# Lockstep head groups in a chunked RWKV-7 scan: 16 heads in two groups, one chunk apart

## The chip, the cores and the metric

The kernel runs on one core of a Trainium2 chip. TensorE (PE) multiplies on a 128 x 128 array, DVE, ACT and POOL work on vectors, SP issues DMAs. Time is device microseconds of one execution; runs of a kernel are compared by their median. TensorE's granted clock is given as a share of 2.4 GHz, so 0.50 is 1.2 GHz.

## The reference

A two-layer decoder trunk: 512 positions, width 1024. The first layer has another mixer and a dense feed-forward part; the second has the RWKV-7 time mixing that the change is about, and eight experts of which each position uses two.

```python
# rwkv7_time_mix: 16 heads of 64; state s is 64 x 64 per head
x = h + dx * mix[i]                      # six token-shifted inputs
r, k, v = xr @ w_r, xk @ w_k, xv @ w_v
w_log = -softplus(-(w0 + tanh(xw @ w1) @ w2)) - 0.5
a = sigmoid(a0 + (xa @ a1) @ a2);  g = sigmoid(xg @ g1) @ g2
kk = normalize(k * k_k);  k = k * (1 + (a - 1) * k_a);  decay = exp(-exp(w_log))
def step(s, (r_t, w_t, k_t, v_t, kk_t, b_t)):
    s = s * w_t[None, :] - (s @ kk_t)[:, None] * b_t[None, :] + v_t[:, None] * k_t[None, :]
    return s, s @ r_t
# then: normalize each head's output, scale and shift, add a bonus (r . k . r_k) v, times g, @ w_o
```

## The kernel before

`rwkv` (L599) runs the recurrence in eight chunks of 64 positions (C), for two head groups (hf = 0 and 1) of eight heads. Inside a chunk the dependence of the positions on each other is a triangular 64 x 64 system per head; its inverse is made ahead of the scan.

*Key stage.* For each of eight column tiles n, `key1` makes the key product and ACT (L789, L790) and DVE (L791, L792) scale it; `sums` (L802) and `key2` normalize; `bonus_z` on POOL (L822) and `bonus` (L829) make the bonus; `key3` decays keys and receptances, with L842 on POOL for tiles 0 to 5 and on DVE for 6 and 7. `flip` multiplies a chunk's keys by their decay to the chunk's end on POOL (L850, four tiles of 128 columns at a time), `flop` transposes the result and stores it for the scan.

*Scores and inverse.* `scores(th)` makes the score products of chunks 4 th to 4 th + 3 (L978). The masks of chunks 0 to 3 are applied as DVE evacuates; those of chunks 4 to 7 by `mask` on POOL (L1002 and L1003, eight pairs). `invert(th)` solves 32 x 32 blocks on DVE, 31 steps of up to four instructions (L1020, L1024) and two transposes (L1027, L1029); it is run a few steps at a time between other work. `merge` joins 32 x 32 blocks to 64 x 64 with 2 x 64 small products (L1045, L1062).

*The scan.* For chunk c (64 positions, on partitions 0 to 63 or 64 to 127 as c is even or odd: its natural half) of one group:

- `step1`: products with the state S (L1159, 4 of 128 columns) and with the values (L1164, one per head) go into one accumulator; ACT copies it to Z (L1169);
- `step2`: one product per head with the inverse (L1177); ACT copies it into the other half of the value tile vu (L1181);
- `step3`: state products (L1193; heads alternate between column halves of the array); DVE adds the decayed state SP (L1199, two per chunk; L1201, a copy, in chunk 0); POOL multiplies S by the next decay to SP (L1206);
- `step4`: output products (L1213); ACT copies the result to Y (L1223).

An f32 product is two records in the trace. `slot(s)` issues the steps one group at a time: group 0 on chunk s, group 1 between chunk s - 1's later steps and chunk s's earlier ones. Behind each step `fill` issues some products of a queue of other work: value products (L883) of the second half until they are done, then gate products (L1262 to L1264), from slot 6 on output products (L1321). Generators of side work (the inverse, the masks, the merge, the norms) advance by one after each step. `norm` normalizes 128 positions of a group: on POOL L1242, L1233 and L1234, on DVE L1236, L1237, L1244, L1252 to L1255, on ACT L1241 and L1245. `load_vu` and `load_kt` fetch the next chunk's values and keys (four and three buffers).

The order in the source is not final: a scheduler orders the instructions of all engines by priorities, and `after` pins one instruction behind another. An accumulator bank holds 512 f32 columns; the kernel rotates through eight.

Of the kernel before, what the change touches and what calls it, by code (L numbers as in the profile page):

```python
# [103 lines left out]
class Trunk:  # L104
# [494 lines left out]
    def rwkv(self, hpool):  # L599
# [502 lines left out]
        for j, _ in enumerate(scores(1)):  # L1102
            run(inv, 3)
            if j < NTT:
                flops(next(v3), 1)
            if j == NTT:
                run(v3)
                for i in range(NTT):
                    t = self.t()
                    nc.scalar.activation(t, pv[i], AF.Copy, scale=cm[:, 0:1])  # L1110
                    nc.sync.dma_start(v_d[i * 128:(i + 1) * 128, 0:512], t)
# [40 lines left out]

        def step1(chains):
            for hf, c in chains:
                p_ = PYZ[hf] = self.ps()
                if c:
                    for j in range(4):
                        n = hf * 4 + j
                        nc.tensor.matmul(p_[:, j * 128:(j + 1) * 128], RK[n].rearrange(flat)[:, c * 128:(c + 1) * 128],  # L1159
                                         Sb[(c - 1) % 2][:, n], start=(j == 0), stop=False, skip_group_check=True)  # L1160
            for hd, hs in enumerate(heads):
                for hf, c in chains:
                    nat, opp = sides(c)
                    mm = nc.tensor.matmul(PYZ[hf][opp, hs], AK[hf][c // 2][nat, hd], VU[hf, c][nat, hs],  # L1164
# [916 lines left out]
```

## Time and profile before

| | |
|---|---|
| Median of 3 runs | 1504.39 us (1502.3 to 1504.78) |
| Profiled execution | 1497.78 us |
| Its span | 1496.1 us |
| Mean granted clock | 0.957 |
| Busy PE / DVE / ACT / POOL | 1418.3 / 987.4 / 796.6 / 334.0 us |
| The scan | 858.3 to 1006.4 us |

Durations in the rows come from the profiled execution. A row of the timeline joins instructions of one line that stand next to each other; its length runs to the modelled end of the last, so the distance from one row's start to the next tells the pace. Idle time in brackets is that of the engine just before, with what ended it. A slot here is the stretch from one group 0 chunk's first state product to the next.

### The profile page before, as it was taken

The numbers are of one execution on the slowest core, as the hardware profiler recorded it, in microseconds if no ns is written. First come the engines' busy times: TensorE is split into PE (matmuls) and PEld (weight loads), VectorE is DVE, ScalarE is ACT, GpSimd is POOL, SyncE is SP. The second block draws the span as 40 slices with busy tenths as digits, with TensorE's granted clock in tenths as the row PEclk, the third lists the DMA queues.
The fourth block names the chain that finished last, engine by engine and source line by source line (L and its number), as shares of the span: only waits on it lengthen the run. The fifth ranks groups of instructions, "written<-read, shape, count | busy, mean of one in ns | idle before, by whom it ended". The sixth has DMA issues, their size and how long they took to land. (4 is left out here: it accounts for less than half of the span.)

```text
span 1496.1 us, 31249 instructions
## 1 busy us (share of the span) xinstructions
PE 1418.3 (95%) x12563; PEld 1121.0 (75%) x12563; DVE 987.4 (66%) x1661; ACT 796.6 (53%) x1262; POOL 334.0 (22%) x357
## 2 busy tenths in 40 slices
PE   7999999999999999999978899898999999999995
PEld 5776788888888444744555569776889989999994
DVE  6643564444444433596767992556899998898894
ACT  4842444322322322495549333334678888888872
POOL 4000002000000013102442612533233323421323
PEclk9999999999999999999989578699999999999998
DMA  4220222232223433242133132236889999999993
GB/s 171 85 71 28 85 85 88 96 99 89 95 99 95 118 104 92 71 159 95 57 106 117 53 103 59 63 124 218 323 283 379 371 396 372 366 366 389 349 342 128
DMA packets 77397, 253.91 MB, mean 170 GB/s; under 512 B 9162, under 2 KB 9290, under 8 KB 77244
## 3 DMA queue, kind: packets, MB, share of 16 engines
q1 hardware_dynamic: 70112, 233.34, 44.4%
q0 software_dynamic: 3136, 10.62, 2.3%
q10 hardware_dynamic: 3996, 7.88, 1.4%
q8 instruction: 100, 1.64, 0.5%
q14 instruction: 53, 0.43, 0.1%
HBM read 235.65 MB, written 16.16 MB: 168 GB/s over the span
## 5 line engine op out<-in xcount | busy, mean ns | idle before, releaser
L226 ACT ACTIVATE whi<-wraw 128x1024 fp32r<-128x1024 f32 x95 | 100.6, 1059 | 269.9 <-PE ps L264 126.0
L264 PE MATMUL ps<-xg,whi 128*128 128x512 f32 x544 | 217.1, 400 | 3.8 <-DVE cs L191 3.4
L263 PE MATMUL ps<-xg,whi 128*128 128x512 f32 x544 | 217.0, 399 | 1.0 <-ACT xg L325 1.0
L265 PE MATMUL ps<-xg,wlo 128*128 128x512 f32 x544 | 216.4, 398 | 0.0
L1741 DVE SCALAR_TENSOR_TENSOR wlo<-eraw,wlo 128x1024 f16<-128x1024 f32 x125 | 154.0, 1232 | 13.7 <-ACT wlo L1740 13.6
L1741 DVE SCALAR_TENSOR_TENSOR whi<-eraw,whi 128x1024 f16<-128x1024 f32 x124 | 152.5, 1230 | 13.7 <-ACT whi L1740 13.4
L227 DVE TENSOR_TENSOR wlo<-wraw,whi 128x1024 fp32r<-128x1024 f32 x95 | 118.6, 1249 | 48.9 <-ACT whi L226 47.7
L1740 ACT ACTIVATE wlo<-eraw 128x1024 f16<-128x1024 f32 x125 | 131.9, 1055 | 20.7 <-PE ps L1820 11.0
L1740 ACT ACTIVATE whi<-eraw 128x1024 f16<-128x1024 f32 x124 | 130.7, 1054 | 15.6 <-PE ps L1820 11.6
L1920 POOL TENSOR_TENSOR hh<-su,hh 128x138 f16<-128x138 f32 (+5 forms) x77 | 82.0, 1066 | 217.7 <-ACT hh L1919 215.6
L1820 PE MATMUL ps<-xe,whi 128*128 128x138 f16 (+6 forms) x704 | 126.8, 221 | 3.6 <-DVE whi L1741 2.9
L1818 PE MATMUL ps<-xe,whi 128*128 128x138 f16 (+6 forms) x704 | 127.7, 221 | 0.0
L1819 PE MATMUL ps<-xe,whi 128*128 128x138 f16 (+6 forms) x704 | 127.5, 221 | 0.0
L1819 PE MATMUL ps<-xe,wlo 128*128 128x138 f16 (+6 forms) x704 | 127.2, 221 | 0.3 <-ACT xe L1610 0.3
L1818 PE MATMUL ps<-xe,wlo 128*128 128x138 f16 (+6 forms) x704 | 127.3, 221 | 0.0
L1820 PE MATMUL ps<-xe,wlo 128*128 128x138 f16 (+6 forms) x704 | 126.7, 220 | 0.4
L264 PEld LDWEIGHTS ps<-xg,whi 128*128 128x128 f32 x544 | 103.0, 189 | 31.1 <-DVE xg L326 6.5
L263 PEld LDWEIGHTS ps<-xg,whi 128*128 128x128 f32 x544 | 103.4, 190 | 25.5 <-ACT xg L325 1.3
L265 PEld LDWEIGHTS ps<-xg,wlo 128*128 128x128 f32 x544 | 103.1, 190 | 24.1 <-issue 0.5
L1820 PEld LDWEIGHTS <-whi 128*128 128x128 f16 x1008 | 97.8, 97 | 8.6 <-DVE whi L1741 5.8
L286 POOL TENSOR_TENSOR tmp<-tmp 128x512 f32<-128x512 f32 x21 | 34.8, 1656 | 300.1 <-ACT tmp L284 247.2
L1820 PEld LDWEIGHTS <-wlo 128*128 128x128 f16 x1016 | 98.6, 97 | 2.4 <-DVE wlo L1741 1.6
(516 smaller groups left out, 3467.9 us busy)
## 6 DMA issues: line engine op xcount, KB each, us to landing
eraw<-in_e_w SPq DMA_DIRECT2D x260, 512.0 KB, 7.3
wraw<-in_ffn_g SPq DMA_DIRECT2D x22, 512.0 KB, 3.4
wraw<-in_ffn_u SPq DMA_DIRECT2D x22, 512.0 KB, 3.3
wraw<-in_ffn_d SPq DMA_DIRECT2D x16, 512.0 KB, 3.6
wraw<-in_w_oo SPq DMA_DIRECT2D x13, 512.0 KB, 3.4
wraw<-in_w_mo SPq DMA_DIRECT2D x8, 512.0 KB, 3.2
wraw<-in_w_rk SPq DMA_DIRECT2D x8, 512.0 KB, 3.3
wraw<-in_w_k SPq DMA_DIRECT2D x8, 512.0 KB, 3.4
```

What stands on the lines that cost most here:

```text
L226: nc.scalar.activation(hi, raw, AF.Copy)
L227: nc.vector.tensor_sub(lo, raw, hi.bitcast(F32))
L263: nc.tensor.matmul(ps, hi[:, j], xh, start=(k == 0), stop=False)
L264: nc.tensor.matmul(ps, hi[:, j], xl, start=False, stop=False)
L265: last = nc.tensor.matmul(ps, lo[:, j], xh, start=False, stop=(k == ktot - 1))
L286: self.nc.gpsimd.tensor_add(sq, sq, parts.pop())
L1740: nc.scalar.activation(w[:, 0], raw, AF.Copy, scale=2048.0)
L1741: low = nc.vector.scalar_tensor_tensor(w[:, 1], raw, 2048.0, w[:, 0], op0=OP.mult, op1=OP.subtract)
L1818: nc.tensor.matmul(ps, w[:, 0, j], x[:, 0, k], start=(k == 0), stop=False)
L1819: nc.tensor.matmul(ps, w[:, 0, j], x[:, 1, k], start=False, stop=False)
L1820: nc.tensor.matmul(ps, w[:, 1, j], x[:, 0, k], start=False, stop=(k == n - 1))
L1920: nc.gpsimd.tensor_sub(hh[:, 1, f], u, hh[:, 0, f])
```

## The change

`slot` becomes a lockstep: in slot s group 0 works on chunk s and group 1 on chunk s - 1, so that their natural halves are opposite, and the products of both alternate head by head in L1178 (value products, was L1164), L1201 (was L1177) and L1237 (was L1213). The value products become a step of their own, `step0`, issued for the next slot's chunks behind `step2`; a product with the identity (L1173) opens their accumulator. `step2` writes both groups into one bank, `step3` (L1217, was L1193) too. There are nine slots instead of eight and a piece. The S adds are now L1223 and L1225, the SP multiply L1230, Z's and VU's copies L1193 and L1205, Y's L1247, the state products L1189.

Fills go in two places of a slot, five and three at a time (two and two in slots 4 and 5, twelve and six in 6 and 7, six and six in 8). The eight mask pairs (now L1018, L1019) leave the start of the scan: they are issued in slots 2 to 6, each behind an SP multiply. In the key stage group 0's key decay is multiplied on ACT (L857, one per tile) instead of POOL; `key3` is split, its last two multiplies becoming `key4`; the L842 multiplies of tiles 4 and 5 go from POOL to DVE; the value preparation runs one key step earlier, and the first inverse two steps at a time instead of three under the second scores.

```diff
-            (nc.gpsimd if n < KD - 2 else nc.vector).tensor_mul(a, a, kk)
+            (nc.gpsimd if n < 4 else nc.vector).tensor_mul(a, a, kk)
+
+        def key4(n):
...
-            nc.gpsimd.tensor_mul(s_, blk, PE[:, n4, c:c + 1].to_broadcast([128, 4, 128]))
+            if hf:
+                nc.gpsimd.tensor_mul(s_, blk, PE[:, n4, c:c + 1].to_broadcast([128, 4, 128]))
+            else:
+                for j in range(4):
+                    nc.scalar.activation(s_[:, j], blk[:, j], AF.Copy, scale=PE[:, j, c:c + 1])
...
-            for k in ((), (0,), (1, 2), (3,), (4, 5), (6,), (7,), ())[n]:
+            for k in ((0,), (1,), (2, 3), (4,), (5, 6), (7,), (), ())[n]:
...
-            nc.gpsimd.tensor_mul(z, z, msk[:, 0:1, :].to_broadcast([128, 8, C]))
+            after(nc.gpsimd.tensor_mul(z, z, msk[:, 0:1, :].to_broadcast([128, 8, C])), turned[0])
...
-            run(inv, 3)
+            run(inv, 2)
...
+        def step0(chains):
+            for hf, c in chains:
+                PYZ[hf, c] = self.ps()
+                nat, opp = sides(c)
+                nc.tensor.matmul(PYZ[hf, c][nat, 0:2], self.ident[nat, opp], self.ident[nat, 0:2], start=True, stop=False,
+                                 skip_group_check=True)
+            for hd, hs in enumerate(heads):
+                for hf, c in chains:
+                    nat, opp = sides(c)
+                    mm = nc.tensor.matmul(PYZ[hf, c][opp, hs], AK[hf][c // 2][nat, hd], VU[hf, c][nat, hs],
+                                          start=(hd == 0), stop=False, skip_group_check=True)
+            return mm
...
-            pu = {hf: self.ps() for hf, c in chains}
+            pu = self.ps()
...
-                    mm = nc.tensor.matmul(pu[hf][opp, hs], NT[i // 2][opp, (i % 2) * 16 + hf * 8 + hd], Z[hf][opp, hs],
+                    mm = nc.tensor.matmul(pu[opp, hs], NT[i // 2][opp, (i % 2) * 16 + hf * 8 + hd], Z[hf][opp, hs],
...
-        def slot(s, gs, count, rate):
-            for f, hf, c in ((step1, 0, s), (step3, 1, s - 1), (step2, 0, s), (step4, 1, s - 1),
-                             (step3, 0, s), (step1, 1, s), (step4, 0, s), (step2, 1, s)):
...
+        def chain(s):
+            return [(hf, s - hf) for hf in range(NH) if 0 <= s - hf < NCH]
+
+        def slot(s, gs, counts, rate):
+            now, nxt = chain(s), chain(s + 1)
...
+            mm = step1(now)
+            for hf, c in nxt:
+                load_vu(hf, c)
+                load_kt(hf, c)
+            fill(mm, counts[0])
+            side()
+            mm = step2(now)
+            if nxt:
+                mm = step0(nxt)
+            side()
+            fill(mm, counts[1])
+            step3(now)
+            side()
+            mm = step4(now)
+            side()
+            fill(mm, counts[2])
...
+            run(mk, (0, 0, 1, 2, 2, 2, 1, 0, 0)[s])
-            if s == 1:
+            if s == 4:
                 fill(None, 96 - vdone[0])
...
-            slot(s, ([inv, mk], [inv, mk], [inv, mk], [join], [norms[0, 0], norms[0, 1]], [norms[1, 0], norms[1, 1]], [norms[2, 0]], [norms[2, 1]], [norms[3, 0]])[s],
-                 (2, 1, 1, 1, 1, 1, 4, 4, 4)[s], 1)
+            slot(s, ([inv], [inv], [inv], [join], [norms[0, 0], norms[0, 1]], [norms[1, 0], norms[1, 1]], [norms[2, 0]], [norms[2, 1]], [norms[3, 0]])[s],
+                 ((5, 3, 0), (5, 3, 0), (5, 3, 0), (5, 3, 0), (2, 2, 0), (2, 2, 0), (12, 6, 0), (12, 6, 0), (6, 6, 0))[s], (2, 2, 2, 2, 1, 1, 1, 1, 1)[s])
```

Before, TensorE goes through the scan one group at a time; at 901 to 906 us, the end of slot 2 (ps is an accumulator, S the state, RK receptances and keys, ak, bs and nt the masked scores and the inverse; x8 counts f32 products):

```order
L1193 MATMUL ps<-vu,kt 64x64 x8
L1159 MATMUL ps<-S,RK 128x128 x4
L1164 MATMUL ps<-vu,ak 64x64 x8
L1213 MATMUL ps<-vu,bs 64x64 x8
L1177 MATMUL ps<-tmp,nt_6449 64x64 x8
```

In the kernel after, the same kinds in slot 0, with numbers: vu_6706 is group 0's next chunk, vu_6710 group 1's first.

```order
L1201 MATMUL ps_6727<-tmp_6704,nt0_6470 64x64 x8
L1173 MATMUL ps_6737<-ident_82 64x2
L1173 MATMUL ps_6739<-ident_82 64x2
L1178 MATMUL ps_6737<-vu_6706,ak_5738 64x64
L1178 MATMUL ps_6739<-vu_6710,ak_5740 64x64
L1178 MATMUL ps_6737<-vu_6706,ak_5738 64x64
```

The value products of two groups have become neighbours and go into two accumulators in turn, right behind L1201. From slot 3 to slot 4 (L1078 are products of the merge):

```order
L1217 MATMUL ps<-vu,kt 64x64 x8
L1078 MATMUL ps<-nt_6469,tmp 32x32 x32
L1237 MATMUL ps<-vu,bs 64x64 x4
L1217 MATMUL ps<-vu,kt 64x64 x8
L1237 MATMUL ps<-vu,bs 64x64 x12
L1078 MATMUL ps<-nt_6469,tmp 32x32 x32
L1189 MATMUL ps<-S,RK 128x128 x8
```

Each L1217 block is one group's, L1237 and L1189 are both groups'; only output and merge products stand between the state products and the L1189 that reads the state.

DVE, at the first copy of the state, before (X, xs: the second inverse; 88 of its instructions stand ahead of the copy):

```order
L1024 TENSOR_TENSOR X<-X,xs 128x5x21
L1020 TENSOR_TENSOR xs<-xs,X 128x5x22 x2
L1024 TENSOR_TENSOR X<-X,xs 128x5x22 x2
L1201 COPY S<-ps 64x4x64 x2
L1020 TENSOR_TENSOR xs<-xs,X 128x5x23
L1020 TENSOR_TENSOR xs<-xs,X 128x4x23
```

After, where 96 instructions of the inverse stand ahead of the copy:

```order
L1036 TENSOR_TENSOR xs<-xs,X 128x4x24 x2
L1040 TENSOR_TENSOR X<-X,xs 128x4x24 x2
L1225 COPY S<-ps 64x4x64 x2
L1036 TENSOR_TENSOR xs<-xs,X 128x4x25
L1036 TENSOR_TENSOR xs<-xs,X 128x3x25
```

And after, at the next S adds, group 0's L1223 for chunk 1 and group 1's copy L1225 for chunk 0:

```order
L1036 TENSOR_TENSOR xs<-xs,X 128x31
L1040 TENSOR_TENSOR X<-X,xs 128x31
L1043 STREAM_TRANSPOSE xs<-X 128x32x32
L1045 STREAM_TRANSPOSE xs<-X 128x32x32
L1070 COPY nt_6469<-xs 32x32x32 x2
L1223 TENSOR_TENSOR S<-ps,SP 64x4x64 x2
L1225 COPY S<-ps 64x4x64 x2
```

The first copy has moved eight inverse instructions back. The next adds, which stood between two steps of the inverse before, now stand behind its end and its two transposes.

POOL at the start of the scan, before (the last mask pairs, then the SP multiplies and the first norm):

```order
L1003 TENSOR_TENSOR bs<-bs,msk 128x512
L1002 TENSOR_TENSOR ak<-ak,msk 64x512
L1003 TENSOR_TENSOR bs<-bs,msk 128x512
L1206 TENSOR_TENSOR SP<-S,pe 64x256 x14
L1242 TENSOR_TENSOR bs<-bs,xn 128x512
L1206 TENSOR_TENSOR SP<-S,pe 64x256 x2
L1233 TENSOR_TENSOR tmp<-tmp,bon 128x512
```

After, there:

```order
L1391 TENSOR_TENSOR A_6699<-wraw,X 128x1024
L1230 TENSOR_TENSOR SP<-S,pe 64x256 x6
L1018 TENSOR_TENSOR ak<-ak,msk 64x512
L1019 TENSOR_TENSOR bs<-bs,msk 128x512
L1230 TENSOR_TENSOR SP<-S,pe 64x256 x4
```

And after, in slot 4, with two norms (L1266, L1257, L1258):

```order
L1019 TENSOR_TENSOR bs<-bs,msk 128x512
L1018 TENSOR_TENSOR ak<-ak,msk 64x512
L1019 TENSOR_TENSOR bs<-bs,msk 128x512
L1266 TENSOR_TENSOR bs<-bs,xn 128x512 x2
L1257 TENSOR_TENSOR tmp<-tmp,bon 128x512
L1258 TENSOR_TENSOR tmp<-tmp,xn 128x512
L1257 TENSOR_TENSOR tmp<-tmp,bon 128x512
```

The masks have moved from ahead of the first SP multiply to places between later ones.

## Rows read from the trace of the kernel before

**Rows 1.** The page, its parts 1 and 2: busy time by engine, and the granted clock of TensorE in 40 slices (tenths of full speed).

```profile
PE 1418.3 (95%) x12563; PEld 1121.0 (75%) x12563; DVE 987.4 (66%) x1661; ACT 796.6 (53%) x1262; POOL 334.0 (22%) x357
...
PEclk9999999999999999999989578699999999999998
```

**Rows 2.** The table of windows, one per slot of the scan; slots 0, 1, 2, 4, 5 and 6 and the sum over all eight stand here. Columns: window, length, busy time of PE, PEld, DVE, ACT, POOL with counts, granted clock, DMA share, GB/s.

```profile
858.30:878.00 19.70, 17.86 (x141) 10.99 (x141) 19.61 (x73) 6.45 (x9) 3.62 (x4) 0.80 0.31 101
878.00:894.60 16.60, 16.59 (x140) 13.24 (x141) 14.43 (x42) 3.15 (x6) 4.30 (x6) 0.69 0.24 77
894.60:906.20 11.60, 11.60 (x149) 9.78 (x147) 7.27 (x11) 5.35 (x8) 3.81 (x4) 1.00 0.36 109
...
927.70:945.20 17.50, 14.08 (x162) 12.83 (x161) 9.14 (x15) 6.37 (x12) 9.10 (x9) 0.79 0.23 76
945.20:963.80 18.60, 17.22 (x141) 15.71 (x141) 11.09 (x18) 4.46 (x9) 11.19 (x12) 0.50 0.24 72
963.80:987.80 24.00, 24.00 (x184) 19.78 (x184) 11.92 (x18) 8.67 (x14) 6.20 (x6) 0.83 0.13 36
...
sum 148.10, PE 141.45 PEld 117.31 DVE 86.29 ACT 51.53 POOL 48.91; mean PE 17.68 PEld 14.66 DVE 10.79 ACT 6.44 POOL 6.11
```

**Rows 3.** The timeline of TensorE in slot 2, granted clock 1.00. Columns: start, length, engine, line, form, count, and in brackets the idle time before it and what ended that.

```profile
901.33 0.69 PE L1193 MATMUL ps<-vu,kt 128*64 128x64 f32 x16
901.95 1.16 PE L1159 MATMUL ps<-S,RK 128*128 128x128 f32 x8
903.03 1.14 PE L1164 MATMUL ps<-vu,ak 64*64 64x64 f32 x16
904.11 1.14 PE L1213 MATMUL ps<-vu,bs 128*64 128x64 f32 x16
```

**Rows 4.** The same view in slot 5, granted clock 0.50.

```profile
947.19 1.97 PE L1164 MATMUL ps<-vu,ak 64*64 64x64 f32 x16
949.09 1.12 PE L1193 MATMUL ps<-vu,kt 128*64 128x64 f32 x16
950.14 1.65 PE L1177 MATMUL ps<-tmp,nt 64*64 64x64 f32 x13
```

**Rows 5.** Groups of TensorE instructions by line over the whole scan, 858.3 to 1006.4 us: count, busy time and mean ns of one, idle time before them.

```profile
L1213 PE MATMUL ps<-vu,bs 128*64 128x64 f32 x256 | 23.0, 250 | 1.4 <-ACT vu L1181 1.4
L1164 PE MATMUL ps<-vu,ak 64*64 64x64 f32 x256 | 22.7, 252 | 0.0
L1177 PE MATMUL ps<-tmp,nt 64*64 64x64 f32 x256 | 21.7, 245 | 0.0
```

**Rows 6.** The same view, ACT.

```profile
L1169 ACT ACTIVATE tmp<-ps 64x512 f32<-64x512 f32 x16 | 9.5, 592 | 49.7 <-PE ps L1164 49.7
```

**Rows 7.** The same view, DVE.

```profile
L1199 DVE TENSOR_TENSOR S<-ps,SP 64x256 f32<-64x256 f32 x24 | 10.1, 421 | 32.9 <-PE ps L1193 32.5
L1027 DVE STREAM_TRANSPOSE xs<-X 128x1024 f32<-128x1024 f32 x1 | 2.0, 1956 | 0.0
```

**Rows 8.** The timeline of TensorE behind the scan: output products.

```profile
1015.96 0.63 PE L1321 MATMUL ps<-whi,bs 128*128 128x512 f32 x2
1016.43 0.39 PE L1321 MATMUL ps<-wlo,bs 128*128 128x512 f32 x1
```

**Rows 9.** Three pieces of the timeline of TensorE: value products in slot 0 and in the key stage, and merge products in slot 3.

```profile
871.27 2.75 PE L883 MATMUL ps<-whi,xn 128*128 128x512 f16 x12
...
756.49 2.72 PE L883 MATMUL ps<-whi,xn 128*128 128x512 f16 x6
...
908.41 1.19 PE L1045 MATMUL ps<-xs,A 32*32 32x32 f32 x32
```

**Rows 10.** The timeline at the end of slot 0: POOL and TensorE behind the first state.

```profile
877.49 1.40 POOL L1206 TENSOR_TENSOR SP<-S,pe 64x256 f32<-64x256 f32 x2 [15.93 <-DVE S L1201]
...
878.01 1.13 PE L1159 MATMUL ps<-S,RK 128*128 128x128 f32 x8 [1.86 <-DVE S L1201]
```

**Rows 11.** Groups by line: DVE's inverse from 806 to 832.2 us; the same line from 843 to 862; POOL from 836 to 862; POOL from 906.2 to 1006.4.

```profile
L1020 DVE TENSOR_TENSOR xs<-xs 128x110 f32<-128x110 f32 (+35 forms) x61 | 14.6, 310 | 2.4 <-POOL xs L1014 2.4
...
L1020 DVE TENSOR_TENSOR xs<-xs,X 128x30 f32<-128x30 f32 (+10 forms) x14 | 10.2, 785 | 2.2 <-POOL X L1014 2.2
...
L1002 POOL TENSOR_TENSOR ak<-ak,msk 64x512 f32<-64x512 f32 x8 | 11.1, 1385 | 14.2 <-DVE msk L1116 13.9
L1003 POOL TENSOR_TENSOR bs<-bs,msk 128x512 f32<-128x512 f32 x8 | 10.3, 1282 | 0.3
...
L1234 POOL TENSOR_TENSOR tmp<-tmp,xn 128x512 f32<-128x512 f32 x7 | 10.9, 1556 | 0.5
L1206 POOL TENSOR_TENSOR SP<-S,pe 64x256 f32<-64x256 f32 x14 | 10.5, 747 | 20.8 <-DVE S L1199 20.2
L1233 POOL TENSOR_TENSOR tmp<-tmp,bon 128x512 f32<-128x512 f32 x7 | 7.3, 1043 | 5.3 <-DMA tmp<-v_d 5.3
```

**Rows 12.** The key stage: two pieces of TensorE's timeline, and POOL's group of L850 from 745 to 760 us.

```profile
748.70 1.09 PE L802 MATMUL ps<-tmp,indw 128*64 128x128 f32 x8 [2.37 <-ACT tmp L789]
...
754.76 1.87 PE L829 MATMUL ps<-indr,tmp 128*128 128x2 f32 x8 [4.65 <-POOL tmp L822]
...
L850 POOL TENSOR_TENSOR xs<-KB,pe 128x512 f32<-128x512 f32 x4 | 6.3, 1606 | 0.8 <-DVE KB L843 0.8
```

**Rows 13.** The DMA view from 840 to 1010 us: destination and source, queue, count, KB each, median us to landing.

```profile
vu<-v_d SPq DMA_DIRECT2D x12, 128.0 KB, 2.5
```

More of the change, by code (lines that the diff above doesn't have):

```diff
@@ L1079, in rwkv @@
         run(v2)
+        vw = [self.half(I["w_vk"][1, kp]) for kp in range(2)]
         inv = invert(0)
         run(inv, 4)
-        vw = [self.half(I["w_vk"][1, kp]) for kp in range(2)]
         vdone, pw = [0], {}
@@ L1102, in rwkv @@
         for j, _ in enumerate(scores(1)):
-            run(inv, 3)
+            run(inv, 2)
             if j < NTT:
                 flops(next(v3), 1)
-            if j == NTT:
+            if j == NTT - 1:
                 run(v3)
[L1108 to L1111, printed above, removed]
                 vw += [self.half(I["w_vk"][1, kp]) for kp in (2, 3)]
-            if j > NTT:
+            if j >= NTT:
+                i = j - NTT
+                t = self.t()
+                nc.scalar.activation(t, pv[i], AF.Copy, scale=cm[:, 0:1])
+                nc.sync.dma_start(v_d[i * 128:(i + 1) * 128, 0:512], t)
                 fill(None, 6)
@@ L1158, in step1 @@
                         n = hf * 4 + j
[L1159 to L1164, printed above, removed]
[L1165 to L1166 removed]
+                        mm = nc.tensor.matmul(p_[:, j * 128:(j + 1) * 128], RK[n].rearrange(flat)[:, c * 128:(c + 1) * 128],
+                                              Sb[(c - 1) % 2][:, n], start=False, stop=False, skip_group_check=True)
                 opp = sides(c)[1]
                 Z[hf] = self.t()
[L1169 removed]
+                nc.scalar.activation(Z[hf][opp], p_[opp], AF.Copy)
             return mm
         def step2(chains):
[L1173 removed]
+            pu = self.ps()
             for hd, hs in enumerate(heads):
@@ L1273, in rwkv, with side @@
         PG, ready = {}, set()
-        def slot(s, gs, count, rate):
-            for f, hf, c in ((step1, 0, s), (step3, 1, s - 1), (step2, 0, s), (step4, 1, s - 1),
-                             (step3, 0, s), (step1, 1, s), (step4, 0, s), (step2, 1, s)):
-                if not 0 <= c < NCH:
-                    continue
-                mm = f([(hf, c)])
-                if mm is not None:
-                    fill(mm, count)
-                if f is step1 and c + 1 < NCH:
-                    load_kt(hf, c + 1)
-                    load_vu(hf, c + 1)
+        turned = [None]
+        def chain(s):
+            return [(hf, s - hf) for hf in range(NH) if 0 <= s - hf < NCH]
+        def slot(s, gs, counts, rate):
+            now, nxt = chain(s), chain(s + 1)
+            def side():
                 for g in gs:
                     run(g, rate)
+            mm = step1(now)
[14 more added lines that the diff above has]
+            fill(mm, counts[2])
         def half(a):
@@ L1342, in out0 @@
             yield from out_mm(0, A, done)
-        for hf in range(NH):
-            load_vu(hf, 0)
-            load_kt(hf, 0)
+        load_vu(0, 0)
+        load_kt(0, 0)
         for mm in merge(0):
@@ L1349, in rwkv @@
             run(inv, 1)
+        step0(chain(0))
         g2 = [scp.tile([128, D], F32R, name=name, bufs=2) for name in ("X", "A21")]
@@ L1374, in rwkv @@
                 join = merge(1)
-            if s == 4:
-                run(mk)
-                run(join)
             if s == 6:
```

36 lines of the change are left out of this document (23 added, 13 removed).

## Prediction

> **What bounds the kernel now.** I read the page first: TensorE has work in 1418.3 us, 95% of the span, and the slices of its granted clock sag from the nineteenth to the twenty-second [rows 1]. The change touches the stretch that ends there, so next came the table of windows, one per slot of the scan [rows 2]. The scan runs from 858.3 to 1006.4 us: 148.1 us in eight slots of 11.6 to 24.0. TensorE's busy time in them sums to 141.45 us, so it waits only 6.65 us; but the granted clock is 0.50 in all of slot 5 (its lower level, 1.2 GHz) and 0.69 to 0.83 in slots 0, 1, 4 and 6, a mixture with 2.4 GHz. So the scan is bound by TensorE, partly at its lower level, and what shortens it is fewer TensorE microseconds.
>
> The TensorE timeline says what a product costs. At full clock the 16 records of L1164 begin 1.08 us before the next kind, 67 ns a record. The 16 records of L1193, whose heads go in turn to the two halves of the array's columns, take 0.62 us, 39 ns each; eight records of L1159 take 1.08 [rows 3]. At 1.2 GHz L1164 takes 1.90 us, 119 ns a record, and L1193 1.05, 66 ns [rows 4]. So neighbours on opposite halves overlap. Groups by line over the scan: L1213 23.0, L1164 22.7, L1177 21.7 us, 67.4 us in all that run on one side today [rows 5].
>
> **The change, part by part. Pairing.** The two head groups now work on neighbouring chunks, whose natural halves are opposite, and the products of a pair alternate between them. L1213 alternates column halves, as L1193 does; L1164 and L1177 alternate row and column halves together. At L1193's pitch the 67.4 us become 67.4 × 39/67 = 39 us, 28 less, if the clock is as before. Bounds for the form that no row shows (both halves alternate): 67 ns, no gain, and 39; I take 39, as L1193 is the nearest row.
>
> One rule speaks against a third of this. The Trainium skill (TensorE: Matmul & The Clock Gate, "The mechanism") says that a weight load overlaps matmuls in flight only where the row group differs. By it L1213's pairs, which differ in columns alone, would gain nothing, and the 28 us would be 18. L1193 differs in columns alone too and goes at 39 against 67 ns [rows 3]: the trace disagrees, and the sum keeps all three.
>
> **Waits that lockstep adds.** Before, a group's evacuation lay under the other group's products; now both wait together. Each link has two ACT copies of 0.59 us (L1169 and its like L1181 [rows 6]) and four S adds of 0.42 us on DVE [rows 7]. Z (1.2 us) lies under five fill products in slots 0 to 3 and twelve in slots 6 and 7; VU under the next step's value products (32 × 39 ns = 1.24 us) and more fills; S (1.7 us) only under L1213's 1.24. That leaves about 0.7 us for S in each slot, and about 1 us more for Z in slots 4 and 5, where two fills (0.235 us each, from L1321's spacing [rows 8]) are all that covers it.
>
> **A slot.** At full clock: state products 2 × 1.08, L1193's 1.24, three pairs at 1.24, eight fills at 0.22 (twelve took 2.75 us with the last one's end [rows 9]) = 1.8, wait 0.7: 9.6; as fills late in the slot cover part of the wait, 9. At 1.2 GHz: 4.2 + 4 × 2.1 + 8 × 0.43 (six took 2.72 us [rows 9]) = 16.
>
> **Slots 0 and 1.** Today POOL waits 15.93 us for the first S copy, and TensorE's L1159 behind it 1.86 us [rows 10]: DVE has 88 instructions of the second inverse in front of it, and the earlier ones ran beside POOL's mask multiplies, L1020 at 785 ns in the mean instead of 310 [rows 11]. The sixteen masks (1385 and 1282 ns, 21 us) leave this place, so the 26 inverse instructions that ran beside them shrink from 20 us to some 6. The new order puts the copy behind 96 inverse instructions, which at 0.2 to 0.25 us from 844 on end near 866. Slot 0: 856.3 to 868, 11.5 us. Slot 1's S waits for the other 26 inverse instructions (5.2 us), two transposes (1.96 each [rows 7]), and two copies and its adds, some 3 us: to about 879, 11 us. Slot 2: 12, between 9 and 16, as TensorE waited before it.
>
> **Slot 3** carries the 256 merge products (32 took 1.19 us at full clock [rows 9], so twice that at the lower): 9 + 9 = 18 to 16 + 15 = 31. I take 22, nearer the full clock.
>
> **Slots 4 and 5.** POOL holds two mask pairs (2 × 2.67), two norms (1.56 and 1.04 of L1234 and L1233, and L1242 between them, 1.3) and four SP multiplies of 0.75 [rows 11]: 5.3 + 7.8 + 3.0 = 16 us. The next S add needs the SP behind them, so I take 16.5 each, whatever the clock. **Slots 6 to 8:** 18 output products × 0.235 = 4.2 us instead of the value products, four gate products and one norm: 15, 12, and 8.5 for the last, which has one group. Sum: 11.5 + 11 + 12 + 22 + 33 + 15 + 12 + 8.5 = 125, against 148.1.
>
> **Before the scan.** The key stage holds two TensorE waits: 2.37 us for ACT's L789, and 4.65 us for the bonus products behind POOL's L822; the L850 multiplies between them take 1.6 us each [rows 12]. Four of these leave POOL for ACT, but eight ACT copies of 128 columns now stand ahead of the last key tile's L789: between 0.15 us (a quarter of 0.59 [rows 6]) and 0.59, so 1.2 to 4.7 us; I take 0.3 and 2.4, half of it in ACT's idle time. Bounds −7 (both waits gone) to +3; I take −2. The L842 multiplies of two tiles more on DVE (at 0.42 to 0.8 us), the value preparation one key step earlier and the slower inverse rate I cost at nothing, as TensorE's waits there end with ACT and POOL; without that cover they cost 1.5. The scan runs from 856.3 to 981.3: its end is 25 us earlier.
>
> **After the scan.** 48 output products remain instead of 32: 16 × 0.235 = 3.8 us. Between nothing (all under the last norm's chain) and 3.8, I charge 2. **SP:** per slot two vu and two kt loads; a vu takes 2.5 us to land [rows 13], is issued behind the state products and needed by step0 some 3 us later: nothing, or up to 1 us a slot where it stands behind a kt. Sum: −25 + 2 = −23.
>
> The profiled run took 1497.78 us (span 1496.1): it would become 1475. The median of the runs is 1504.39, 6.6 above it; there the forecast is 1504.4 − 23 = 1481. All slots at full clock and POOL not in the way: 11.5 + 11 + 9 + 18 + 11 + 11 + 13 + 11 + 8 = 103.5, so −44.6, with the same edges (−2 and +2): 1460. All at the lower level: 13 + 16 + 16 + 31 + 17 + 17 + 21 + 19 + 14 = 164, so +16: 1520.
>
> **Rivals.** (a) *The clock stays high and POOL is not in the way.* For: the pairing packs TensorE's work, and slot 2 had 1.00 [rows 2]. Against: more waits for both groups. Half-way between the forecast and the full-clock bound: 1470. Chance 0.17.
>
> (b) *POOL becomes the bound from slot 2 on.* For: it has 21 us more inside slots 2 to 6, between the SP multiplies, and DVE beside its masks ran at 785 instead of 310 ns [rows 11]. Against: slots 4 and 5 have them in the sum already. If each of slots 2 to 6 is 3 us longer: 1496. Chance 0.14.
>
> (c) *L1177's pairs do not overlap*, since both groups now write one accumulator bank from opposite row halves. No row of before shows two row halves going into one bank; L1193 shows two column halves in one. 28 ns a record at full clock, 53 at the lower, times 32 records, eight slots: 7 to 14 us; 1491. Chance 0.10. The Trainium skill (TensorEngine Tiling (Array Packing), "Gotcha 1: PSUM Pressure") says that different row tiles can't access the same bank simultaneously; by it this rival would be the forecast. No trace here shows it.
>
> (d) *Slower: lockstep leaves TensorE idle at every link.* Both groups wait for Z, VU and S at once, TensorE stops three times a slot, and stays at 1.2 GHz. For: each slot of the scan in which TensorE waited over a microsecond (0, 4 and 5) is followed by one at 0.50 to 0.83 [rows 2]. Against: the fills in slots 0 to 3 and 6 to 8. It decides from a mean slot of 16.5 us on (148.1 in nine slots); all at the lower level it is 18.2. The middle of 1504 and 1520: 1512. Chance 0.10. Late loads alone, 1 to 3 us a slot, I put at 1500, chance 0.04.
>
> **The numbers.** Forecast 1481 (its own range 1474 to 1488) 0.45, (a) 0.17, (b) 0.14, (c) 0.10, (d) 0.10, late loads 0.04. A difference under 0.2%, 3 us, can't be told from none here. Faster: 0.45 + 0.17 + 0.14 + 0.10 less 0.02 from the tail of (b) = 0.84; within: 0.05, the late loads and half of that tail; slower: 0.11, (d) and the rest. The range 1464 to 1503 leaves out the far end of (a) and nearly all of (d).
>
> **What would show it.** L1178, L1201 and L1237 at 39 ns a record at full clock; L1201 at 67 would be (c). The S copy of slot 0 near 866. POOL busy nearly throughout slots 4 and 5; if in slots 2 and 3 too, (b). Slots near 11.5, 11, 12, 22 and 16.5 us. The waits at L802 and L829 2 us shorter in sum. The forecast is wrong if the granted clock is 0.50 in more than three slots, or if L1189 waits more than 2 us for S in most.

## The result, and the profile after

The changed kernel takes 1464.32 us (1460.0 to 1469.44, four runs) against 1503.35 of before: ratio 0.9748, interval 0.9702 to 0.9794, some 38 us faster where 23 were forecast. It lies 0.3 us above the lower end of the range, 1464, and below the 1474 to 1488 of the forecast itself. The profiled execution's span fell from 1496.1 to 1459.2 us, by 36.9. The page after, the two lines that answer to [rows 1]:

```profile
PE 1375.9 (94%) x12601; PEld 1086.7 (74%) x12601; DVE 974.9 (67%) x1663; ACT 805.2 (55%) x1290; POOL 322.2 (22%) x348
...
PEclk9999999999999999999999769898999999999998
```

TensorE's share hardly moves, its time falls by 42 us, and the sag of the clock is shorter. The table of windows, one row per slot 0 to 8, beside [rows 2]:

```profile
855.20:866.00 10.80, 10.77 (x111) 7.59 (x110) 5.00 (x22) 1.18 (x2) 0.42 (x1) 0.57 0.01 2
866.00:878.20 12.20, 8.99 (x148) 7.26 (x148) 10.74 (x33) 6.23 (x9) 2.11 (x4) 0.86 0.42 121
878.20:886.50 8.30, 8.18 (x158) 6.55 (x157) 5.43 (x7) 4.60 (x7) 4.73 (x6) 1.00 0.59 163
886.50:902.85 16.35, 16.35 (x414) 14.49 (x413) 6.42 (x11) 10.00 (x16) 10.12 (x12) 1.00 0.43 131
902.85:914.10 11.25, 8.45 (x160) 7.24 (x157) 6.46 (x10) 5.67 (x11) 11.09 (x9) 1.00 0.45 129
914.10:932.40 18.30, 11.36 (x161) 9.56 (x159) 13.20 (x17) 5.30 (x10) 17.23 (x16) 0.82 0.23 73
932.40:949.60 17.20, 16.32 (x187) 14.11 (x185) 12.72 (x21) 6.88 (x12) 10.89 (x10) 0.79 0.23 71
949.60:960.50 10.90, 10.70 (x137) 8.98 (x136) 7.79 (x13) 6.10 (x10) 6.13 (x5) 1.00 0.25 86
960.50:967.40 6.90, 6.90 (x56) 5.55 (x56) 4.04 (x6) 4.19 (x8) 2.32 (x2) 1.00 0.68 211
sum 112.20, PE 98.01 PEld 81.32 DVE 71.79 ACT 50.14 POOL 65.04; mean PE 10.89 PEld 9.04 DVE 7.98 ACT 5.57 POOL 7.23
```

The scan starts 3.1 us earlier and takes 112.2 us instead of 148.1; what follows it is 2.1 us longer: −3.1 − 35.9 + 2.1 = −36.9. TensorE's busy time in it falls by 43.4 us and its waiting grows from 6.65 to 14.2. Times by line over the scan, beside [rows 5]:

```profile
L1189 PE MATMUL ps<-S,RK 128*128 128x128 f32 x112 | 17.4, 310 | 4.2 <-DVE S L1223 4.2
L1178 PE MATMUL ps<-vu,ak 64*64 64x64 f32 x256 | 13.5, 242 | 0.0
L1201 PE MATMUL ps<-tmp,nt 64*64 64x64 f32 x256 | 12.9, 238 | 0.0
L1237 PE MATMUL ps<-vu,bs 128*64 128x64 f32 x256 | 12.0, 234 | 0.0
```

The three lines take 38.4 us where they took 67.4: 29 of the 43.4 us. (Where lines interleave their times overlap, so lines sum to more than TensorE's busy time.) Another 5.7 are output products (23.3 us before, 17.6 now), of which 60 records stood in the scan and 48 do now; the rest is spread over the other lines. TensorE's timeline in slots 2 and 4, where the clock is 1.00, and the waits, beside [rows 3]:

```profile
881.28 1.09 PE L1201 MATMUL ps<-tmp,nt 64*64 64x64 f32 x30
882.16 0.27 PE L1178 MATMUL ps<-vu,ak 64*64 64x64 f32 x2
...
882.33 0.98 PE L1178 MATMUL ps<-vu,ak 64*64 64x64 f32 x28
883.24 0.82 PE L890 MATMUL ps<-whi,xn 128*128 128x512 f16 x3
...
909.06 0.69 PE L1217 MATMUL ps<-vu,kt 128*64 128x64 f32 x16
909.57 1.10 PE L1237 MATMUL ps<-vu,bs 128*64 128x64 f32 x32
...
874.48 0.93 PE L1217 MATMUL ps<-vu,kt 128*64 128x64 f32 x16 [3.18 <-ACT vu L1205]
...
913.48 0.69 PE L1217 MATMUL ps<-vu,kt 128*64 128x64 f32 x16 [2.81 <-DVE S L1223]
914.10 1.16 PE L1189 MATMUL ps<-S,RK 128*128 128x128 f32 x8
...
918.40 1.44 PE L1189 MATMUL ps<-S,RK 128*128 128x128 f32 x8 [3.14 <-DVE S L1223]
...
930.78 1.12 PE L1217 MATMUL ps<-vu,kt 128*64 128x64 f32 x16 [3.80 <-DVE S L1223]
```

28 records of L1178 begin 0.91 us before the next kind, 32 ns each, and 30 of L1201 0.88 us, 29 ns each; 32 of L1237 take 1.10 us to the last one's end, where 16 took 1.14 before. Four waits, in slots 1, 4 and 5, make up 12.9 of the 14.2 us. What makes the S adds late in slots 4 and 5 is shown by DVE's timeline in slot 5:

```profile
926.77 3.18 DVE L1277 TENSOR_TENSOR bs<-bs,gvar 128x512 f32<-128x512 f32 x2 [1.28 <-POOL bs L1266]
929.88 0.85 DVE L1223 TENSOR_TENSOR S<-ps,SP 64x256 f32<-64x256 f32 x2
...
933.79 1.10 DVE L1278 TENSOR_TENSOR bs<-bs,tmp 128x512 f32<-128x512 f32 x1 [1.16 <-POOL tmp L1258]
934.91 0.86 DVE L1223 TENSOR_TENSOR S<-ps,SP 64x256 f32<-64x256 f32 x2
```

The chain of waits over slots 4 to 6 (start, length, what it runs through) goes through POOL at the same place:

```profile
919.79 1.27 POOL ak L1018
921.06 1.74 POOL bs L1019
...
925.51 2.45 POOL bs L1266 x2
927.96 1.46 POOL tmp L1257
```

An S add waits in DVE's order behind a norm's L1277 or L1278, which waits for POOL, which has a slot's masks ahead of that norm.

### The profile page after: what moved, and what is told of

It reads as the page before. It is cut to its first block, busy times and chain, and to the rows that moved or that the text cites. A ratio compares the mean times of both kernels' runs of the same rounds, so it can differ in the third digit from the quotient of the medians.

```text
span 1459.2 us, 31329 instructions
## 1 busy us (share of the span) xinstructions
PE 1375.9 (94%) x12601; PEld 1086.7 (74%) x12601; DVE 974.9 (67%) x1663; ACT 805.2 (55%) x1290; POOL 322.2 (22%) x348
## 4 chain that ended last, share of the span: by engine, by line
PE 79%; DVE 9%; DMA 3%; ACT 3%; POOL 3%; issue 2%; DVEq 0%; ACTq 0%; SPq 0%; POOLq 0%
PE ps L264 9%; PE ps L263 8%; PE ps L265 8%; PE ps L1858 7%; PE ps L1857 7%; PE ps L1856 7%; PE ps L245 3%; PE ps L246 3%; PE ps L247 3%; PE ps L1359 2%; PE ps L890 2%; DMA eraw<-in_e_w 2%; PE ps L278 1%; PE ps L760 1%; PE ps L762 1%
## 5 line engine op out<-in xcount | busy, mean ns | idle before, releaser
L1779 DVE SCALAR_TENSOR_TENSOR whi<-eraw,whi 128x1024 f16<-128x1024 f32 x124 | 152.7, 1232 | 13.8 <-ACT whi L1778 13.5
```

What stands on the lines that cost most here:

```text
L1779: low = nc.vector.scalar_tensor_tensor(w[:, 1], raw, 2048.0, w[:, 0], op0=OP.mult, op1=OP.subtract)
```

## Experiments

Twelve more kernels were run. Theory A of the first four says that the overlap of paired products carries most of the gain, theory B that the masks' move and the earlier inverse do. The scan's length, clock and TensorE busy time are those of one profiled execution each; the ratio is that of the timed runs.

| kernel | ratio to before (interval) | scan us | clock | PE busy |
|---|---|---|---|---|
| before | 1 | 148.1 | 0.80 | 141.45 |
| changed | 0.9748 (0.9702–0.9794) | 112.2 | 0.88 | 98.01 |
| e1_unpaired | 0.9789 (0.9764–0.9815) | 120.45 | 0.92 | 110.51 |
| e2_masks_first | 0.9751 (0.9732–0.9771) | 114.5 | 0.92 | 91.64 |
| e3_decay_pool | 0.9761 (0.9742–0.9781) | 111.5 | 0.90 | 96.78 |
| e4_before_masks | 0.9959 (0.9938–0.9979) | 144.1 | 0.85 | 136.16 |
| e5_inv2 | 0.9739 (0.9705–0.9772) | 113.4 | 0.88 | 97.51 |
| e6_masks224 | 0.9716 (0.9679–0.9753) | 108.9 | 0.92 | 93.25 |
| e7_values_now | 0.9675 (0.9642–0.9707) | 107.5 | 0.93 | 94.41 |
| e8_outputs_first | 0.9824 (0.9786–0.9862) | 124.45 | 0.86 | 100.57 |
| e9_now_masks | 0.9704 (0.9687–0.9721) | 111.4 | 0.92 | 98.26 |
| e11_adds_first | 0.9714 (0.9689–0.9739) | 106.4 | 0.91 | 96.08 |
| e12_now_unpaired | 0.9812 (0.9794–0.9830) | 123.8 | 0.87 | 118.74 |
| e13_inverse_end | 0.9673 (0.9643–0.9704) | 105.65 | 0.94 | 94.44 |

Where the scan begins varied from 854 to 863 us among kernels with nearly the same code ahead of it, so I read the scan's length for mechanisms and the ratio for what a part is worth. What follows the scan varied too, from 485 to 493 us, so the two need not agree.

**e1_unpaired.** In `step0`, `step2` and `step4`:

```diff
-            for hd, hs in enumerate(heads):
-                for hf, c in chains:
+            for hf, c in chains:
+                for hd, hs in enumerate(heads):
```

> The changed kernel with only the alternation undone: in the value, inverse and output products the eight heads of one group come first and then the eight of the other; steps, fills, masks and waits stay in lockstep. Theory A (most of the gain is the overlap of neighbouring products on opposite halves): the three lines go back from 30 to 61-67 ns a record at full clock, TensorE's busy time in the scan grows by about 25 us, of which some falls into its 14 us of waits: 18 to 28 us slower than the changed kernel, ratio to before 0.986 to 0.994. Theory B (the gain comes from the masks' move and the earlier inverse): within 4 us of the changed kernel, ratio 0.972 to 0.978.

Measured: 6 us slower than the changed kernel by the ratios (0.0041 × 1503), between the two theories, and 8 in the scan. The two intervals overlap, so the 6 us are not clear of noise. Its groups by line over the scan:

```profile
L1178 PE MATMUL ps<-vu,ak 64*64 64x64 f32 x256 | 18.0, 239 | 0.0
L1189 PE MATMUL ps<-S,RK 128*128 128x128 f32 x112 | 17.8, 317 | 0.5 <-DVE S L1225 0.5
L1237 PE MATMUL ps<-vu,bs 128*64 128x64 f32 x256 | 16.7, 229 | 0.0
L1201 PE MATMUL ps<-tmp,nt 64*64 64x64 f32 x256 | 16.6, 227 | 0.0
```

And two rows of its timeline at the end of slot 7, clock 1.00:

```profile
969.52 1.85 PE L1237 MATMUL ps<-vu,bs 128*64 128x64 f32 x32
971.30 1.16 PE L1189 MATMUL ps<-S,RK 128*128 128x128 f32 x8
```

The three lines take 51.3 us: without alternation they have already lost 16 of the 29 us. Two blocks of 16 that stand next to each other take 1.78 us to the next kind, where two separate ones took 2 × 1.08 [rows 3]; that is 0.38 us for each of 3 lines in 7 slots, 8 us by this estimate. The rest of the 16 I put down to the clock, 0.92 instead of 0.80; no run isolates it. Alternation proper takes off the other 12.9, at a clock of 0.88. So e1, which lacks only the alternation, is already some 32 of the 38 us faster than before: the larger part comes with lockstep itself, and no run takes that apart further than e2 to e4 do for the masks and the key decay.

**e2_masks_first and e4_before_masks.** e2 takes the masks back to the scan's start, without their pins behind an SP multiply:

```diff
-            run(mk, (0, 0, 1, 2, 2, 2, 1, 0, 0)[s])
...
-            slot(s, ([inv], [inv], [inv], [join],
+            slot(s, ([inv, mk], [inv, mk], [inv, mk], [join],
```

e4 makes their move alone in the kernel before, with the pins:

```diff
-            slot(s, ([inv, mk], [inv, mk], [inv, mk], [join],
+            run(mk, (0, 0, 1, 2, 2, 2, 1, 0, 0)[s])
...
+            slot(s, ([inv], [inv], [inv], [join],
```

> The changed kernel with the sixteen mask multiplies back at the start of the scan, beside the second inverse, as before. Theory A: the inverse is contended again and ends about 15 us later (near 886 instead of 871 us), slot 1 grows by 8 to 15 us, slots 4 and 5 lose 3 to 6 each: in sum 2 to 9 us slower than the changed kernel, ratio 0.976 to 0.981. Theory B: 18 us or more slower, ratio 0.987 or above.

> The kernel before with one part of the change alone: the masks spread over slots 2 to 6 behind the SP multiplies. Theory A: the first S copy comes near 865 instead of 877 us, slot 0 loses its 1.9 us wait and some of its clock; the rest of the scan is still bound by one-sided products: 2 to 9 us faster than before, ratio 0.994 to 0.999. Theory B: 18 us or more faster, ratio 0.988 or below.

Measured: e4 is 6 us faster than before, as theory A had it. e2 equals the changed kernel (ratio 0.9751), where theory A asked for 2 to 9 us more. Theory B falls. But e2's draw has two sides. Its timeline at the end of slot 0:

```profile
880.78 2.08 PE L1189 MATMUL ps<-S,RK 128*128 128x128 f32 x8 [12.44 <-DVE S L1225]
```

Its window over slots 4 to 6, columns as in [rows 2]:

```profile
917.13:956.14 39.01, 31.31 (x502) 26.57 (x500) 29.24 (x45) 17.76 (x33) 26.19 (x23) 1.00 0.34 101
```

With the masks beside the inverse TensorE waits 12.4 us for the first S copy; without them in slots 4 to 6 these take 39.0 us instead of 46.75, at full clock. The move saved one and paid the other.

**e3_decay_pool.** Group 0's `flip` on POOL again:

```diff
-            if hf:
-                nc.gpsimd.tensor_mul(s_, blk, PE[:, n4, c:c + 1].to_broadcast([128, 4, 128]))
-            else:
-                for j in range(4):
-                    nc.scalar.activation(s_[:, j], blk[:, j], AF.Copy, scale=PE[:, j, c:c + 1])
+            nc.gpsimd.tensor_mul(s_, blk, PE[:, n4, c:c + 1].to_broadcast([128, 4, 128]))
```

> The changed kernel with group 0's key decay on POOL again; the split of the key step stays. If ACT's multiplies are what started the scan 3.1 us earlier: 2 to 4 us slower, ratio 0.976 to 0.978, and TensorE's wait for L822 returns to about 4.6 us. If the split key step and the earlier value preparation did it: no change within 1 us.

Measured: the ratio is 0.9761, 2 us slower and inside the interval of the changed kernel. TensorE waits 5.57 us for L822 where the changed kernel waits 3.00 and the kernel before 4.65, but no longer the 1.08 us for L789 at L802 that the changed kernel has. The two waits together are 7.02 us before, 5.57 in e3 and 4.08 in the changed kernel: of what these two waits lost, ACT's multiplies took about half and other parts of the change the other half. The time can't settle it.

**e5_inv2.** Under the first merge's products:

```diff
-            run(inv, 1)
+            run(inv, 2)
```

> The changed kernel with the second inverse run two steps instead of one between the merge's products, so that the first S copies stand some ten instructions further back in DVE's order. Theory C (in slots 0 and 1 DVE holds the inverse back behind an S copy that waits 5.7 us for TensorE, and slot 1's 3.2 us wait for VU follows): the inverse ends near 866 instead of 871 us, slot 1 loses 3 us and more of low clock: 3 to 5 us faster than the changed kernel, ratio 0.971 to 0.974. Rival: the late S copy costs in slot 0 what slot 1 gains: no change within 1 us.

Measured: no change (0.9739). The 3.2 us wait for VU went, and 2.72 us for Z came before it, also on ACT. The rival holds, by another wait than it named. It is a weak test of theory C: the S copies still waited 3.05 us for TensorE with the inverse's last steps behind them, and its first transpose began only 1.2 us earlier, at 869.71 us.

**e6_masks224.** The mask pairs earlier:

```diff
-            run(mk, (0, 0, 1, 2, 2, 2, 1, 0, 0)[s])
+            run(mk, (0, 2, 2, 4, 0, 0, 0, 0, 0)[s])
```

> The changed kernel with the mask pairs in slots 1, 2 and 3 (two, two, four) instead of 2 to 6. Theory D (POOL bounds slots 4 and 5, with 28 of 29.6 us busy): these two slots lose 10.5 us of POOL work, TensorE's waits there (2.8, 3.1, 3.8 us) mostly go: 5 to 9 us faster than the changed kernel, ratio 0.969 to 0.972. Rival (DVE's norm chain bounds them): within 2 us of the changed kernel.

Measured: the ratio is 0.9716, 5 us faster; the intervals overlap. Slots 1 and 4 to 6 in its table of windows:

```profile
873.50:889.70 16.20, 8.68 (x149) 7.01 (x149) 14.97 (x32) 6.19 (x9) 7.15 (x8) 0.79 0.29 91
...
914.40:925.35 10.95, 8.87 (x159) 7.50 (x157) 6.43 (x10) 5.67 (x11) 8.11 (x7) 1.00 0.43 131
925.35:938.70 13.35, 9.22 (x161) 7.78 (x159) 10.41 (x17) 5.31 (x10) 11.32 (x11) 1.00 0.33 99
938.70:953.60 14.90, 13.34 (x186) 11.28 (x184) 12.55 (x19) 6.78 (x12) 7.71 (x8) 1.00 0.26 82
```

Slots 4 to 6 take 39.2 us instead of 46.75, as in e2. That is theory D's size, but its waits did not mostly go: they fall from 10.6 to 7.8 us (7.7 in e2), nearly all still for S behind DVE's norms. The other 4.7 us are TensorE time at a clock of 1.00 where slots 5 and 6 had 0.82 and 0.79. So both theory D and its rival hold in part. Slot 1 gives 4 us back (16.2 against 12.2), where TensorE waits 7.49 us for VU; its masks run beside the end of the inverse.

**e7_values_now and e8_outputs_first.** Two parts of the change undone, each alone: the value products in front of their own slot's state products, and the output products in front of the next state's:

```diff
-            mm = step1(now)
+            step0(now)
+            mm = step1(now)
...
-            if nxt:
-                mm = step0(nxt)
...
-        step0(chain(0))
```

```diff
-            step3(now)
-            side()
             mm = step4(now)
             side()
+            step3(now)
+            side()
```

> The changed kernel with the value products in front of their own slot's state products instead of one step ahead. Theory E (one step ahead they cover the wait for VU, 1.2 us a slot): TensorE waits for ACT's L1205 in every slot, 5 to 12 us slower than the changed kernel, ratio 0.978 to 0.984. Rival (in front of the state products they cover the wait for S instead, which is as long): within 2 us.

> The changed kernel with the output products in front of the next state's products instead of behind them. Theory F (behind the state's products they cover part of the S adds): L1189 waits 1 to 2 us more for S in every slot and the clock falls with it: 6 to 14 us slower than the changed kernel, ratio 0.979 to 0.985. Rival (the S adds are late for DVE's or POOL's sake): within 2 us.

Measured: e7 is faster than the changed kernel, 0.9675 against 0.9748, some 11 us; the intervals just overlap. Neither side of its expectation had that. Placed there the value products cover the S adds, and the fills alone cover VU: slot 4 takes 9.3 us instead of 11.25, its wait for S 0.30 instead of 2.81. VU is waited for over half a microsecond only in slot 1, as in the changed kernel; the largest wait is 6.7 us in slot 6, ahead of group 1's state products. Two rows of TensorE's timeline:

```profile
870.46 0.69 PE L1217 MATMUL ps<-vu,kt 128*64 128x64 f32 x16 [3.09 <-ACT vu L1205]
...
928.23 2.07 PE L1189 MATMUL ps<-S,RK 128*128 128x128 f32 x8 [6.74 <-DVE S L1223]
```

This accounts for less than half of the gain. In the profiled executions e7 is 12.2 us shorter: 4.7 us in the scan, 1.0 ahead of it and 6.5 behind it. Behind the scan DVE waits 6.14 us for a load (of ht) in the changed kernel and 1.80 in e7. The four kernels with the values in their own slot and the pairs kept have 485.3 to 490.0 us behind the scan, the changed kernel, e2, e3, e5 and e6 491.0 to 492.6; why, no run shows.

e8 is 11 us slower than the changed kernel (0.9824), as theory F said, but by 8.49 us of waiting for S at the end of slot 4 and 6.20 for a norm's L1279 at the end of slot 5, not by a little in every slot.

**e12_now_unpaired.** e7 with e1's edit:

```diff
-            for hd, hs in enumerate(heads):
-                for hf, c in chains:
+            for hf, c in chains:
+                for hd, hs in enumerate(heads):
```

> The values in their own slot (e7_values_now), with the alternation undone as in e1_unpaired. Theory G (alternation takes 13 to 17 us of TensorE time out of the scan, of which a part turned into waits and low clock in the changed kernel): where fewer waits are left it shows more fully, 9 to 15 us slower than e7, ratio 0.9735 to 0.9775. Rival (as much is lost in waits here): 4 to 8 us slower than e7, ratio 0.970 to 0.973.

Measured: 21 us slower than e7 (0.9812 against 0.9675), more than theory G asked. In the profiled executions, e12's slowest and e7's fastest, 16.3 us of it are in the scan; 8.5 lie ahead of it and 5.9 behind it, where the edit touches nothing (DVE waits 4.82 us for the load of ht there, 1.80 in e7). So I take the scan's figures: the alternation is worth 8 us in one order and 16 in the other. Of TensorE's time on the three lines it takes 12.9 in the first pair and 18.6 in the second (52.7 to 34.1). What the lower clock costs in the scan can be estimated from the table as length × (1 − clock): 9.6 us in e1 and 13.5 in the changed kernel, but 16.1 in e12 and 7.5 in e7. Taking out the alternated work came with 4 us more of that cost in one pair and 9 less in the other, in one execution each.

**e9_now_masks and e11_adds_first.** e7 with the mask pairs elsewhere:

```diff
-            run(mk, (0, 0, 1, 2, 2, 2, 1, 0, 0)[s])
+            run(mk, (0, 0, 2, 4, 0, 0, 2, 0, 0)[s])
```

e11 also pins the norm's last part:

```diff
-            nc.vector.reciprocal(var, var)
+            after(nc.vector.reciprocal(var, var), added[0])
...
-                        nc.vector.tensor_add(o, pst[d, n4], SP[hf][c][d])
+                        added[0] = nc.vector.tensor_add(o, pst[d, n4], SP[hf][c][d])
```

> The values in their own slot (as in e7_values_now) and the mask pairs in slots 2, 3 and 6 (two, four, two), none in 4 and 5. Theory D (POOL's masks between the SP multiplies and the norms bound slots 4 to 6): the 6.7 us wait of L1189 for S in slot 5 of e7 goes, 4 to 8 us faster than e7, ratio 0.962 to 0.965. Rival (DVE's norm chain bounds them by itself): within 2 us of e7, ratio 0.966 to 0.969.

> As e9_now_masks, and the last part of a norm on DVE (from the reciprocal on) pinned behind the S adds issued before it. Theory H (what is left of TensorE's waits for S in slots 4 to 6 is DVE's norm instructions, one of which waits for POOL, in front of the adds): 2 to 5 us faster than e9, ratio 0.959 to 0.963. Rival (the norms end later and slot 6's output products wait for them): no change or up to 4 us slower than e9.

Measured: neither beats e7 (0.9704, 0.9714). In e9 the 6.74 us wait shrank to 1.50, but slot 3, with four mask pairs, waits 0.7 us for S, its clock is 0.81 and it takes 20.4 us instead of 16.3; slot 6 waits 3.47 for S. The masks and that wait do not explain the clock: in e11 slot 3 has the same four pairs and the same 0.69 us wait, runs at 1.00 and takes 17.2. Slots 4 to 6 together gain only 1.1 us on e7 (43.4 against 44.5), so in this order theory D has little. In e11 no wait for S is above 1.3 us; 4.55 us for the norms' L1279 ahead of the output products took their place, as its rival said.

**e13_inverse_end.** e7, with the transposes that end the second inverse behind slot 1's S adds and copies, and slot 1's side work one step at a time instead of two:

```diff
-            nc.vector.transpose(NTc.rearrange("p n t -> p t n"), N)
+            mm = nc.vector.transpose(NTc.rearrange("p n t -> p t n"), N)
+            if th:
+                after(mm, added[0])
...
-                 ((5, 3, 0), (5, 3, 0), (5, 3, 0), (5, 3, 0), (2, 2, 0), (2, 2, 0), (12, 6, 0), (12, 6, 0), (6, 6, 0))[s], (2, 2, 2, 2, 1, 1, 1, 1, 1)[s])
+                 ((5, 3, 0), (5, 3, 0), (5, 3, 0), (5, 3, 0), (2, 2, 0), (2, 2, 0), (12, 6, 0), (12, 6, 0), (6, 6, 0))[s], (2, 1, 2, 2, 1, 1, 1, 1, 1)[s])
```

> The values in their own slot (e7_values_now), and the two transposes that end the second inverse pinned behind slot 1's S adds and copies, so that ACT's copies that read them stand behind slot 1's VU. Theory J (in slot 1 TensorE waits 3.1 us for VU only because ACT waits for these transposes, and 0.7 us for S): both waits go, slot 1 takes 8 to 9 us instead of 11.6, slot 2 keeps the full clock: 2 to 5 us faster than e7, ratio 0.964 to 0.966. Rival (the transposes and their copies stop slot 2 instead): within 2 us of e7, ratio 0.966 to 0.969.

Measured: the ratio is 0.9673, as in e7. The waits in slot 1 went as said, and it takes 7.9 us, but slot 2 takes 10.5 instead of 8.5, with 0.88 us of waiting for VU and 0.45 for Z. The rival holds.

## Why the prediction was right, and where it was off

The direction, the edges (−3.1 before the scan for −2; +2.1 behind it for +2) and the TensorE time of the three lines (67.4 to 38.4, for 39 forecast) came out. The scan's sum did not: 112.2 us instead of 125. Neither of the two signs of being wrong came: no slot ran at 0.50 throughout, and L1189 waited over 2 us for S in slot 5 alone. Point by point:

- *Pairing, "28 less, if the clock is as before".* The size was right and the cause was half of it. Records go at 29 to 34 ns instead of the 39 I took, since 39 held the step to another form (16 records of L1217 take 0.51 us to L1237, 0.62 to L1189). But e1 shows that only 12.9 of the 29 us are alternation; by the estimates there 8 come with two blocks of a kind standing next to each other, and about 8 are left for the clock, though the sum was made for a clock "as before". That it came out so near 39 is in part luck. By the Trainium skill (TensorE: Matmul & The Clock Gate, "The mechanism"), where a weight load overlaps matmuls in flight only if the row group differs, L1237 would have gained nothing, as its pairs differ in columns alone. The trace disagrees: 32 of its records take 1.10 us at full clock against 1.85 in e1, 12.0 against 16.7 over the scan.
- *Rival (c), one accumulator bank for both row halves.* It fell: L1201 takes 12.9 us, less than L1178, which has two banks. The Trainium skill (TensorEngine Tiling (Array Packing), "Gotcha 1: PSUM Pressure") says that different row tiles can't use one bank at the same time; no cost of it is seen here.
- *The clock.* This is the step that was furthest off. I gave slots 2 and 3 12 and 22 us, between their full-clock bounds (9, 18) and the lower level; both ran at 1.00 and took 8.3 and 16.35. That is 9.35 of the 12.8 us by which the sum was too long: 7 for the clock, the rest for bounds that had too slow a pace and a wait for S. Slots 6 to 8 came out in sum (35.0 for 35.5), slot 6 at 0.79 and 17.2 us for 15. Over the scan the cost of the lower clock, length × (1 − clock), fell from 29.6 us (148.1 × 0.20) to 13.5: 16 us of the 36, by an estimate that no run isolates. I had argued that more waits mean a lower clock, but their sum doesn't tell it: e2 waits 22.9 us (114.5 − 91.64) with a clock of 0.92, the changed kernel 14.2 with 0.88, e12 5.1 with 0.87.
- *Slots 0 and 1.* 22.5 forecast, 23.0 measured, but for other reasons. The inverse began at 837.0, not 844, and its 96 instructions ended at 859.4; the S copy at 865.09 waited 5.7 us for TensorE, not for DVE. In slot 1 the wait was for VU (L1205), behind an ACT copy that waited for the inverse's transpose, a queue that I had not followed:

```profile
865.09 0.87 DVE L1225 COPY S<-ps 64x256 f32<-64x256 f32 x2 [5.74 <-PE ps L1217]
...
872.89 1.06 ACT L1072 ACTIVATE nt<-xs 32x1024 f32<-32x1024 f32 x1 [3.71 <-DVE xs L1043]
```

- *Slots 4 and 5.* 33 forecast as POOL's bound, 29.55 measured (11.25 and 18.3) with POOL busy for 28.3 of it: the mechanism was right. Its price over slots 4 to 6 is 7.6 to 7.7 us in e2 and e6, some 2.9 of it waits and 4.7 TensorE time at a higher clock; in e7's order (e9) it is 1.1.
- *Waits of lockstep.* "About 0.7 us for S in each slot" was wrong in slots 2 and 3 (0.12 us in the two together) and far too small in 4 and 5 (9.8). And the value products "one step ahead", which I counted as VU's cover, are of more use ahead of their own slot's state products: e7's scan is 4.7 us shorter.
- *The other rivals.* (d) fell: the waits doubled, but TensorE's work fell by more, and the clock rose. (b) fell: POOL was busy for 4.7 of 8.3 us in slot 2 and 10.1 of 16.35 in slot 3, and TensorE hardly waited there. Of (a) one half came true, the clock in slots 2, 3, 4, 7 and 8; the other did not, for POOL was in the way in slots 4 and 5.
- *The range.* The interval of the ratio, from 1459 to 1472 us, reaches below the range's 1464, so that the median lies inside it is in part luck.

The kernels e7_values_now and e13 are faster still: e7 takes 1451.97 us, ratio 0.9675. All four kernels with the values in their own slot and the pairs kept lie between 0.9673 and 0.9714, the changed kernel and its neighbours e2, e3, e5 and e6 between 0.9716 and 0.9761.

What stays open: how much of the 36 us the clock gives by itself, since no run holds it; what of lockstep other than the alternation makes the larger part of the gain; and why the time behind the scan differs between kernels.

## What to carry to other kernels

When small products use half of the array, put those of independent work on the other half and next to each other: here alternation took 12.9 us off three lines, and standing next to each other some 8 by an estimate. When everything waits together, place the work that is independent in front of the wait that is longest now, and try its neighbours: such a move made the scan 4.7 us shorter here and doubled what the alternation was worth in it (16 against 8 us, in one execution each). Look also at what lies outside the stretch that was edited, since more than half of a gain can be there. And a multiply on POOL can cost TensorE time where DVE's queue has something waiting for it in front of the critical add.

## What was not expected of the hardware

TensorE's granted clock stayed at 0.50 through a stretch in which it was busy without a pause, after a wait of 12 us. The wait in the changed kernel's timeline, ahead of the scan:

```profile
832.82 1.88 PE L1061 MATMUL ps<-X,A 32*32 32x32 f32 x32 [11.98 <-DVE msk L1132]
```

The window from there to the scan, columns as in [rows 2]:

```profile
832.80:855.20 22.40, 22.39 (x272) 15.24 (x272) 22.23 (x82) 6.80 (x11) 4.45 (x3) 0.50 0.11 37
```

22.39 of 22.40 us are busy, with 32 x 32 and value products in turn, and the clock is at its lower level for all of it; the same kind of merge products in slot 3 ran at 1.00. The kernel before has the same there, after a shorter wait:

```profile
835.92 1.89 PE L1045 MATMUL ps<-X,A 32*32 32x32 f32 x32 [3.60 <-DVE msk L1116]
```

```profile
835.90:858.30 22.40, 22.38 (x272) 15.25 (x272) 20.11 (x22) 6.80 (x11) 21.81 (x17) 0.50 0.11 37
```

So the change made this wait 8.4 us longer (the kernel before has another, of 5.89 us, ending at 823 us), and the clock behind it is the same. What keeps it at its lower level there no run shows, and a kernel without the wait was not tried.
